# A decoder step on one core: the low parts of 44 delta net weight blocks made by an accumulating transfer from GpSimd, with other costs for transfers in the planner and the convolution states moved in fewer transfers

## The chip, the cores and the metric

One NeuronCore of one Trainium2 chip runs the whole program in one launch. TensorE (PE, with its weight loads as PEld) multiplies, VectorE (DVE) and ScalarE (ACT) do elementwise work, GpSimd (POOL) does elementwise work on data outside PSUM, and SyncE (SP) issues transfers. The five have instruction queues of their own, each in order, and wait for each other on semaphores. The metric is the device time of one execution in microseconds (us), the median of several runs; lower is better.

## The reference

A two-layer decoder trunk for a prompt of 512 tokens and 64 sample tokens (8 sequences of 8), T = 576 columns in all, with 1024 channels in fp32. Layer 0 is a pooling mixer and a SwiGLU FFN, layer 1 a gated delta net and a SwiGLU FFN; each sublayer stands between two RMS norms. What matters here is the delta net:

```python
proj = h @ w_in                      # 1024 -> 4096 (q, k, v) + 2048 (z) + 32 (b, a)
qkv_c, new_conv = short_conv(qkv, conv_buf, conv_w)     # causal, width 4, then SiLU
q, k = l2norm(...), l2norm(...)      # 8 heads of 128, each for 2 of the 16 v heads
u = solve(t_mat, v * beta[..., None])                   # unit lower triangular
w = solve(t_mat, kb * jnp.exp(gc)[..., None])
o, s_new = lax.scan(step, s0, xs)    # the state passes from chunk to chunk
o = rms_norm(o, o_norm) * jax.nn.silu(zf)
y = o.reshape(B, L, GDN_V_DIM) @ w_out                  # 2048 -> 1024
```

Beside y the delta net returns the last three rows before the convolution (new_conv) for the prompt and each sample sequence, and the recurrent states.

## The kernel before

**Weight blocks.** Every large product is made of three fp32r matmuls per pair of operands: each operand is split in a high part (rounded to fp32r) and a low part (the rest), and high x high, high x low and low x high are summed in PSUM (`mm3`, L683). A weight block is 1024 rows by 128 columns, held as 128 partitions x 8 x 128. `Weights.load` (L670) has SP fetch it from DRAM into `wraw` (512 KB); `Weights.split` (L675) has ACT copy it, rounded, into `wh`, and then one subtraction `wraw - wh` goes into `wl`, on DVE or on POOL (`EITHER`). `wraw`, `wh` and `wl` have three buffers each (`wts = Weights(ctx, 3, 3)`). One block's 48 matmuls (8 row tiles x 3 x the two halves of the columns, 256 and 320) are in the generator `halves` (L1215).

**The delta net** runs over four groups G of two k heads and four v heads. `project(G)` takes eight weight blocks (two k, two q, four v) through the matmuls, the convolution (`ac`, DVE), the activation (`ACT`) and the norms, and `zproj(h)` takes one block of z; `ZB` says which z blocks go with which group. `core(G)` forms the decay and the triangular matrices, inverts them on DVE (`inv32`, L1117: 31 rounds of a product, `ii<-ia,ii`, and a subtraction, `ii<-ii`, each of which needs the one before), scans over four spans of the prompt and updates the sample states. `out0` (L1726) multiplies the first eight v heads by eight blocks of `w_out` in pairs, beside the last core; the second half of `w_out` follows with the next norm.

**The convolution states.** `project(G)` loads the three rows before the sample tokens for its eight chunks with eight transfers into two `crow` tiles (24 rows a chunk, four chunks on 96 partitions), which PE transposes in two matmuls, and at its end PE transposes the new rows (`nct`) in two, ACT copies them to `nco`, and sixteen transfers store them, eight for the prompt and eight for the samples.

**The order of the work.** All of this is recorded as operations with dependencies, and `Plan.finish` puts them in an order for each engine: list scheduling by a rank, with costs from `Plan.cost` and the engine, port and transfer rules in `Plan.forward`, then 40 rounds in which ranks from a backward pass are stirred at random (with a fixed seed) and the best order is kept. The order is written out before the run; on the chip each engine follows its own list, so that an instruction that waits holds up all behind it on that engine. An operation of `EITHER` goes to POOL only while DVE has enough other work. A transfer cost the SP queue 60 ns there, and 2000 ns and its bytes at 240 bytes per ns to land. Since nearly all instructions are put out by one helper, the profile has one line for them (L302), and tiles are what tells them apart.

Of the kernel before, what the change touches and what calls it, by code (L numbers as in the profile page):

```python
# [11 lines left out]
F32 = mybir.dt.float32  # L12
F32R = mybir.dt.float32r
I32 = mybir.dt.int32
AF = mybir.ActivationFunctionType
ALU = mybir.AluOpType
PSUM = bass.MemoryType.PSUM
DRAM = bass.MemoryType.DRAM
SB = bass.MemoryType.SB

P = 128
D = 1024
NC = D // P
# [33 lines left out]
class Plan:  # L57
# [101 lines left out]
    def cost(self, eng, method, out, ins, k):  # L159

        n = self.size(out)
        if method == "dma_start":
            return 60.0, 2000.0 + n * list(out.ap)[0][1] * 4 / 240.0
# [194 lines left out]
    def forward(self, rank):  # L358
# [65 lines left out]
        while todo:  # L424
# [54 lines left out]
            if e == "DVE" and ops[i][8] or e == "POOL" and ops[i][9] != "memset":  # L479
                other = port["POOL" if e == "DVE" else "DVE"]  # L480
                late = max(other - 130.0 - t, 0.0)
                hold, done = hold + late, done + late
                if e == "DVE" or ops[i][9] == "tensor_tensor":
                    port[e] = t + done
# [33 lines left out]
def hybrid_kernel(  # L518
# [12 lines left out]
        ("PE", nc.tensor), ("ACT", nc.scalar), ("DVE", nc.vector), ("POOL", nc.gpsimd), ("SP", nc.sync)))  # L531
    EITHER = plan.engine(DVE=nc.vector, POOL=nc.gpsimd)
# [132 lines left out]
    class Weights:  # L665
# [3 lines left out]

        def load(self, src, row, col, nk, n=P, eng=EITHER):  # L670
            raw = self.p.tile([P, 8, P], F32, name="wraw", tag="wraw", bufs=self.raw)[:, :nk, :n]
            SP.dma_start(raw, src[row:row + nk * P, col:col + n].rearrange("(k p) m -> p k m", p=P))
            return self.split(raw, eng)

        def split(self, raw, eng=EITHER):  # L675
            _, nk, n = raw.shape
            h = self.p.tile([P, 8, P], F32R, name="wh", tag="wh", bufs=self.bufs)[:, :nk, :n]
            l = self.p.tile([P, 8, P], F32R, name="wl", tag="wl", bufs=self.bufs)[:, :nk, :n]
            ACT.activation(h, raw, AF.Copy)
            eng.tensor_tensor(l, raw, h.bitcast(F32), op=sub)  # L680
            return h, l
# [461 lines left out]
    with ExitStack() as st:  # L1143
# [80 lines left out]
        def project(G, out, zh=()):  # L1224
# [14 lines left out]
            cp = bank("x")[:, :8 * R0].rearrange("p (c r) -> p c r", c=8)  # L1239
            for j4 in range(2):  # L1240

                crow = pp.tile([4 * R0, P], F32, name="crow", tag="crow", bufs=2)
                for j, (_, _, cc) in enumerate(chunks[4 * j4:4 * j4 + 4]):
                    SP.dma_start(crow[j * R0:(j + 1) * R0],
                                 state_gdn_conv[0].rearrange("b r d -> (b r) d")[:, cc * P:(cc + 1) * P])
                PE.transpose(cp[:, 4 * j4:4 * j4 + 4].rearrange("p c r -> p (c r)"), crow, ident[:4 * R0, :4 * R0])
# [57 lines left out]
            for j, (kind, i, cc) in enumerate(chunks):  # L1304
                both = early[j:j + 1]
                yield from halves(wts.load(w_in, 0, cc * P, NC), both)
# [35 lines left out]
            nco = pp.tile([4 * R, 2, P], F32, name="nco", tag="nco", bufs=1)  # L1342
            pn_ = bank("x", (P, 4, P))[:4 * R, :2]
            for j4 in range(2):
                PE.transpose(pn_[:, j4], nct[:, 4 * j4:4 * j4 + 4].rearrange("p c r -> p (c r)"), ident)
            ACT.activation(nco, pn_, AF.Copy)
            for j, (_, _, cc) in enumerate(chunks):
                src = nco[j % 4 * R:(j % 4 + 1) * R, j // 4]
                SP.dma_start(nc_prompt[0, 0, :, cc * P:(cc + 1) * P], src[:CW - 1])
                SP.dma_start(nc_sample[0].rearrange("b r d -> (b r) d")[:, cc * P:(cc + 1) * P], src[CW - 1:])  # L1350

        def zproj(h):

            both = []
            yield from halves(wts.load(w_in, 0, CONV + h * P, NC), both)
# [370 lines left out]
        def out0():  # L1726
# [4 lines left out]
            for m0, m1 in ((0, 2), (2, 4), (4, 6), (6, 8)):  # L1731
                acs = [pp.tile([P, UTOT], F32, name="ac", tag="ac", bufs=ACB) for _ in range(m0, m1)]
                ws = [wts.load(wo, 0, m * P, 8) for m in range(m0, m1)]
# [182 lines left out]
```

## Time and profile before

| what | value |
|---|---|
| time, median of 3 runs (lowest to highest) | 1594.57 us (1593.03 to 1595.5) |
| the profiled execution: its time | 1590.5 us |
| the profiled execution: span from first to last instruction | 1588.8 us |
| first FFN and what is ahead of it | 0 to about 450 us of the span |
| delta net, groups 0 to 3 and `out0` | about 450 to 1110 us |
| second half of `w_out`, second FFN | about 1110 us to the end |
| granted TensorE clock, mean | 0.990 |

A page of the profile gives for each engine the time in which it was busy; matmuls are pipelined and their ends are modelled, so that a busy PE may still have room between two matmuls. A group's row reads: line, engine, operation, out<-in, shapes, count, then busy time and mean duration of one, then the idle time of the engine ahead of it and what ended that. The chain of waits is followed back from the last instruction: at each step to what released it, or to the instruction before it on its engine.

### The profile page before, as it was taken

How to read it: one execution, taken by the hardware profiler on the slowest of the kernel's cores; microseconds unless marked ns; L12 is line 12 of the kernel's file. 1: busy time of each engine (PE TensorE's matmuls, PEld its weight loads, DVE VectorE, ACT ScalarE, POOL GpSimd, SP SyncE). 2: the span in 40 equal slices, each digit the busy share in tenths (PEclk: the TensorE clock that was granted, in tenths of full speed). 3: DMA queues.
4: the chain of work that ended last, by engine and by line, in shares of the span. 5: the costliest groups of instructions: out<-in, count | busy, mean ns of one | idle time of the engine just before them, and what ended most of it. 6: DMA issues, size and time to landing. Idle time of an engine off the chain costs nothing.

```text
span 1588.8 us, 30549 instructions
## 1 busy us (share of the span) xinstructions
PE 1543.5 (97%) x11941; PEld 1479.0 (93%) x11941; DVE 1190.6 (75%) x2377; ACT 797.1 (50%) x1654; POOL 120.9 (8%) x257
## 2 busy tenths in 40 slices
PE   8999999999999999999999999899999999999997
PEld 8999999999999898888898889799999999999997
DVE  6894565678596798897999899658697576766864
ACT  7753443445455956353563664424465453434554
POOL 3210000000010011130211110100010000000000
PEclk9999999999999999999999999899999999999998
DMA  6454323232565432424333433555765423233263
GB/s 182 138 175 123 99 75 102 67 107 78 165 179 159 124 97 81 128 80 117 103 108 101 133 115 113 170 172 145 231 209 156 142 83 91 80 90 115 64 179 104
DMA packets 346463, 197.87 MB, mean 125 GB/s; under 512 B 14087, under 2 KB 339504, under 8 KB 346311
## 3 DMA queue, kind: packets, MB, share of 16 engines
q1 hardware_dynamic: 346319, 195.92, 42.5%
q8 instruction: 94, 1.54, 0.4%
q14 instruction: 50, 0.41, 0.1%
HBM read 165.60 MB, written 30.52 MB: 123 GB/s over the span
## 4 chain that ended last, share of the span: by engine, by line
PE 42%; DVE 16%; ACT 3%; DMA 2%; issue 2%; SPq 0%; POOL 0%; DVEq 0%; ACTq 0%
PE ps_B L302 15%; PE ps_A L302 12%; PE ps_m L302 6%; PE ps_s L302 4%; PE ps_k L302 3%; DVE ac L302 3%; DVE ii L302 2%; DVE ia L302 2%; DVE Uw L302 2%; DVE wl L302 1%; DVE vt L302 1%; PE ps_n L302 1%; DVE QD L302 1%; PE ps_x L302 1%; DVE St L302 1%
## 5 line engine op out<-in xcount | busy, mean ns | idle before, releaser
L302 ACT ACTIVATE wh<-wraw 128x1024 fp32r<-128x1024 f32 (+4 forms) x240 | 233.2, 976 | 246.1 <-PE ps_B L302 89.6
L302 DVE TENSOR_TENSOR wl<-wraw,wh 128x1024 fp32r<-128x1024 f32 (+4 forms) x233 | 259.4, 1118 | 89.9 <-ACT wh L302 42.3
L302 PE MATMUL ps_m<-hH,wh 128*128 128x320 f32 (+1 forms) x832 | 243.9, 311 | 1.2 <-ACT zz L302 0.9
L302 PE MATMUL ps_m<-hL,wh 128*128 128x320 f32 (+1 forms) x832 | 240.2, 306 | 0.0
L302 PE MATMUL ps_m<-hH,wl 128*128 128x320 f32 (+1 forms) x832 | 237.1, 306 | 0.2 <-DVE wl L302 0.2
L302 PEld LDWEIGHTS ps_m<-hH,wh 128*128 128x128 f32 x832 | 154.1, 191 | 6.8 <-issue 1.9
L302 PEld LDWEIGHTS ps_m<-hL,wh 128*128 128x128 f32 x832 | 153.5, 191 | 2.2 <-issue 0.9
L302 PEld LDWEIGHTS ps_m<-hH,wl 128*128 128x128 f32 x832 | 152.7, 191 | 2.6 <-issue 0.9
L302 PE MATMUL ps_B<-hH,wl 128*128 128x320 f32 (+1 forms) x444 | 128.9, 305 | 1.0 <-DVE wl L302 1.0
L302 PE MATMUL ps_B<-hH,wh 128*128 128x320 f32 (+1 forms) x444 | 129.3, 304 | 0.0
L302 PE MATMUL ps_B<-hL,wh 128*128 128x320 f32 (+1 forms) x444 | 128.3, 304 | 0.0
L302 PE MATMUL ps_A<-hH,wh 128*128 128x256 f32 (+1 forms) x432 | 121.1, 291 | 0.7 <-DVE yo L302 0.7
L302 PE MATMUL ps_A<-hL,wh 128*128 128x256 f32 (+1 forms) x432 | 120.8, 290 | 0.0
L302 PE MATMUL ps_A<-hH,wl 128*128 128x256 f32 (+1 forms) x432 | 120.0, 290 | 0.1
L302 PE MATMUL ps_B<-aH,wh 128*128 128x288 f32 x352 | 99.3, 296 | 1.2 <-DVE xa L302 1.2
L302 PE MATMUL ps_A<-aH,wh 128*128 128x288 f32 x352 | 99.0, 297 | 0.7 <-ACT wh L302 0.7
L302 PE MATMUL ps_B<-aL,wh 128*128 128x288 f32 x352 | 99.2, 296 | 0.0
L302 PE MATMUL ps_A<-aL,wh 128*128 128x288 f32 x352 | 99.0, 295 | 0.0
L302 PE MATMUL ps_A<-aH,wl 128*128 128x288 f32 x352 | 98.5, 295 | 0.2 <-DVE wl L302 0.2
L302 PE MATMUL ps_B<-aH,wl 128*128 128x288 f32 x352 | 98.5, 296 | 0.0
L302 PEld LDWEIGHTS ps_B<-hH,wl 128*128 128x128 f32 x444 | 81.8, 188 | 2.4 <-DVE wl L302 2.3
L302 DVE SCALAR_TENSOR_TENSOR ac<-u,cwt,ac 128x600 f32<-128x600 f32 x96 | 80.8, 851 | 2.8 <-ACT ac L302 2.5
(468 smaller groups left out, 4083.4 us busy)
## 6 DMA issues: line engine op xcount, KB each, us to landing
wraw<-in_ffn_w_in_dram SPq DMA_DIRECT2D x77, 512.0 KB
wraw<-in_gdn_w_in_dram SPq DMA_DIRECT2D x56, 512.0 KB
graw<-in_ffn_w_in_dram SPq DMA_DIRECT2D x33, 512.0 KB
wraw<-in_ffn_w_out_dram SPq DMA_DIRECT2D x32, 448.0 KB
wraw<-in_gdn_w_out_dram SPq DMA_DIRECT2D x24, 512.0 KB
wraw<-in_ffn_w_out_dram SPq DMA_DIRECT2D x32, 320.0 KB
St<-in_state_gdn_rec_dram SPq DMA_DIRECT2D x32, 256.0 KB
out_dram<-St SPq DMA_DIRECT2D x32, 256.0 KB
```

Source lines behind the costliest of these rows:

```text
L302: calls[e](*a, **k)
```

## The change

Four things are changed together.

1. `load` and `split` take `dma`. With it, `wl` is made in two steps in place of the subtraction: ACT writes `-wh` into `wl`, and a transfer issued from POOL (`SUM`) adds `wraw` to it, from SBUF to SBUF, 512 KB. It is set for the 24 blocks of `project(1)` to `project(3)`, for the z blocks 4 to 15 and for the eight blocks of `out0`: 44 blocks. Group 0, z blocks 0 to 3, the second half of `w_out` and both FFNs stay as they were. `wraw` is free for the next load only once that transfer has landed, and the matmuls that read `wl` wait for its landing.
2. `Plan.cost` gives a transfer on POOL 1200 ns of its queue and 3500 ns and its bytes at 120 bytes per ns to land; on SP 350 or 400 ns of the queue (2500 ns from DRAM to DRAM) where there were 60. In `Plan.forward` a transfer on POOL doesn't take the port that POOL shares with DVE.
3. The convolution states are loaded with three transfers a group instead of eight and stored with six instead of sixteen. They lie by 24 or 27 rows x 4 chunks x 128, so PE transposes each chunk by itself: eight matmuls in and eight out a group, where there were two and two. `crow` and `nco` share one buffer.
4. With other costs the planner finds another order for the whole program.

```diff
--- before.py
+++ after.py
@@ -160,7 +160,11 @@
 
         n = self.size(out)
         if method == "dma_start":
-            return 60.0, 2000.0 + n * list(out.ap)[0][1] * 4 / 240.0
+            m = n * list(out.ap)[0][1]
+            if eng == "POOL":
+                return 1200.0, 3500.0 + m * 4 / 120.0
+            hold = 2500.0 if out.space == DRAM and ins[0].space == DRAM else 400.0 if m > 16384 else 350.0
+            return hold, 2000.0 + m * 4 / 240.0
         ps = any(x.space == PSUM for x in ins)
         if eng == "PE":
             rows = self.rows(ins[0])
@@ -476,7 +480,7 @@
                 hold *= fast
             taken[i] = True
             todo -= 1
-            if e == "DVE" and ops[i][8] or e == "POOL" and ops[i][9] != "memset":
+            if e == "DVE" and ops[i][8] or e == "POOL" and ops[i][9] not in ("memset", "dma_start"):
                 other = port["POOL" if e == "DVE" else "DVE"]
                 late = max(other - 130.0 - t, 0.0)
                 hold, done = hold + late, done + late
@@ -529,6 +533,7 @@
     plan = Plan(tc)
     PE, ACT, DVE, POOL, SP = (plan.engine(**{name: real}) for name, real in (
         ("PE", nc.tensor), ("ACT", nc.scalar), ("DVE", nc.vector), ("POOL", nc.gpsimd), ("SP", nc.sync)))
+    SUM = plan.engine(POOL=nc.gpsimd)
     EITHER = plan.engine(DVE=nc.vector, POOL=nc.gpsimd)
     mult, add, sub = ALU.mult, ALU.add, ALU.subtract
 
@@ -667,17 +672,21 @@
             self.p = pool("wp", stack=stack)
             self.raw, self.bufs = raw, bufs
 
-        def load(self, src, row, col, nk, n=P, eng=EITHER):
+        def load(self, src, row, col, nk, n=P, eng=EITHER, dma=False):
             raw = self.p.tile([P, 8, P], F32, name="wraw", tag="wraw", bufs=self.raw)[:, :nk, :n]
             SP.dma_start(raw, src[row:row + nk * P, col:col + n].rearrange("(k p) m -> p k m", p=P))
-            return self.split(raw, eng)
-
-        def split(self, raw, eng=EITHER):
+            return self.split(raw, eng, dma)
+
+        def split(self, raw, eng=EITHER, dma=False):
             _, nk, n = raw.shape
             h = self.p.tile([P, 8, P], F32R, name="wh", tag="wh", bufs=self.bufs)[:, :nk, :n]
             l = self.p.tile([P, 8, P], F32R, name="wl", tag="wl", bufs=self.bufs)[:, :nk, :n]
             ACT.activation(h, raw, AF.Copy)
-            eng.tensor_tensor(l, raw, h.bitcast(F32), op=sub)
+            if dma:
+                ACT.activation(l, h.bitcast(F32), AF.Copy, scale=-1.0)
+                SUM.dma_start(l.bitcast(F32), raw, accum_op=add)
+            else:
+                eng.tensor_tensor(l, raw, h.bitcast(F32), op=sub)
             return h, l
 
     def mm3(ps, w, acts, nk, first=True, last=True):
@@ -1237,13 +1246,16 @@
             R0 = (CW - 1) * NB
             cst_t = pp.tile([P, 8, NB, CW - 1], F32, name="cstt", tag="cstt", bufs=1)
             cp = bank("x")[:, :8 * R0].rearrange("p (c r) -> p c r", c=8)
+            runs = ((0, 0, 2), (0, 2, 2), (1, 0, 4))
             for j4 in range(2):
 
-                crow = pp.tile([4 * R0, P], F32, name="crow", tag="crow", bufs=2)
-                for j, (_, _, cc) in enumerate(chunks[4 * j4:4 * j4 + 4]):
-                    SP.dma_start(crow[j * R0:(j + 1) * R0],
-                                 state_gdn_conv[0].rearrange("b r d -> (b r) d")[:, cc * P:(cc + 1) * P])
-                PE.transpose(cp[:, 4 * j4:4 * j4 + 4].rearrange("p c r -> p (c r)"), crow, ident[:4 * R0, :4 * R0])
+                crow = pp.tile([R0 + CW - 1, 4, P], F32, name="crow", tag="crow", bufs=1)[:R0]
+                for _, c, k in (r for r in runs if r[0] == j4):
+                    c0 = chunks[4 * j4 + c][2] * P
+                    SP.dma_start(crow[:, c:c + k], state_gdn_conv[0].rearrange("b r d -> (b r) d")[:, c0:c0 + k * P]
+                                 .rearrange("r (c p) -> r c p", c=k))
+                for c in range(4):
+                    PE.transpose(cp[:, 4 * j4 + c], crow[:, c], ident[:R0, :R0])
             ACT.activation(cst_t.rearrange("p c b r -> p c (b r)"), cp, AF.Copy)
             nct = pp.tile([P, 8, (CW - 1) * (NB + 1)], F32, name="nct", tag="nct", bufs=1)
             if G == 0:
@@ -1303,7 +1315,7 @@
 
             for j, (kind, i, cc) in enumerate(chunks):
                 both = early[j:j + 1]
-                yield from halves(wts.load(w_in, 0, cc * P, NC), both)
+                yield from halves(wts.load(w_in, 0, cc * P, NC, dma=G > 0), both)
                 psA, psB = both
                 if len(pend) == 2:
                     finish(*pend.pop(0))
@@ -1339,20 +1351,22 @@
             for f in pend:
                 finish(*f)
             R = (CW - 1) * (NB + 1)
-            nco = pp.tile([4 * R, 2, P], F32, name="nco", tag="nco", bufs=1)
-            pn_ = bank("x", (P, 4, P))[:4 * R, :2]
             for j4 in range(2):
-                PE.transpose(pn_[:, j4], nct[:, 4 * j4:4 * j4 + 4].rearrange("p c r -> p (c r)"), ident)
-            ACT.activation(nco, pn_, AF.Copy)
-            for j, (_, _, cc) in enumerate(chunks):
-                src = nco[j % 4 * R:(j % 4 + 1) * R, j // 4]
-                SP.dma_start(nc_prompt[0, 0, :, cc * P:(cc + 1) * P], src[:CW - 1])
-                SP.dma_start(nc_sample[0].rearrange("b r d -> (b r) d")[:, cc * P:(cc + 1) * P], src[CW - 1:])
+                pn_ = bank("x", (P, 4, P))[:R]
+                for c in range(4):
+                    PE.transpose(pn_[:, c], nct[:, 4 * j4 + c], ident)
+                nco = pp.tile([R, 4, P], F32, name="nco", tag="crow", bufs=1)
+                ACT.activation(nco, pn_, AF.Copy)
+                for _, c, k in (r for r in runs if r[0] == j4):
+                    cols = slice(chunks[4 * j4 + c][2] * P, (chunks[4 * j4 + c][2] + k) * P)
+                    for dst, src in ((nc_prompt[0, 0], nco[:CW - 1]),
+                                     (nc_sample[0].rearrange("b r d -> (b r) d"), nco[CW - 1:])):
+                        SP.dma_start(dst[:, cols].rearrange("r (c p) -> r c p", c=k), src[:, c:c + k])
 
         def zproj(h):
 
             both = []
-            yield from halves(wts.load(w_in, 0, CONV + h * P, NC), both)
+            yield from halves(wts.load(w_in, 0, CONV + h * P, NC, dma=h >= ZB[1]), both)
             psA, psB = both
             zz = pp.tile([P, T], F32, name="zz", tag="zz", bufs=2)
             ACT.activation(zz[:, :256], psA, AF.Silu)
@@ -1730,7 +1744,7 @@
                 yield 0
             for m0, m1 in ((0, 2), (2, 4), (4, 6), (6, 8)):
                 acs = [pp.tile([P, UTOT], F32, name="ac", tag="ac", bufs=ACB) for _ in range(m0, m1)]
-                ws = [wts.load(wo, 0, m * P, 8) for m in range(m0, m1)]
+                ws = [wts.load(wo, 0, m * P, 8, dma=True) for m in range(m0, m1)]
                 for hf in HALVES:
                     hi, o0, n = hf
                     for i in range(m1 - m0):
```

By count of the instructions in the two built programs, DVE has 114 full-size subtractions `wl<-wraw,wh` where it had 152, POOL 1 where it had 7; ACT has 44 more copies of 128x1024, and four more of 27x512 for the states; PE has 32 + 32 transposes of states where it had 8 + 8 (and 90 fill-in matmuls `ps_w` where it had 86); SP has 563 transfers where it had 623, and POOL 44 where it had none.

The order on DVE in the inversion of group 3 (`ii` is the matrix that is inverted, `ia` its transposed copy, `vs` and `vt` the v heads, `BD`, `TQ`, `ks` the samples' front), before:

```order
L302 TENSOR_TENSOR ii<-ii 128x27x3
L302 TENSOR_TENSOR TQ<-ps_k,des 64x64
L302 TENSOR_TENSOR ii<-ia,ii 128x78
L302 TENSOR_SCALAR vs<-ps_x,nk 64x128
L302 TENSOR_TENSOR ii<-ii 128x26x3
L302 TENSOR_TENSOR wl<-wraw,wh 128x1024
L302 TENSOR_TENSOR ii<-ia,ii 128x100
L302 TENSOR_TENSOR wl<-wraw,wh 128x1024
L302 TENSOR_TENSOR ii<-ii 128x25x4
```

and the same rounds in the change:

```order
L306 TENSOR_TENSOR ii<-ii 128x27x3
L306 TENSOR_TENSOR des<-des,s_in 128x128
L306 TENSOR_TENSOR ii<-ia,ii 128x78
L306 TENSOR_TENSOR vs<-vs,oss 64x512
L306 TENSOR_TENSOR ii<-ii 128x26x3
L306 TENSOR_TENSOR ii<-ia,ii 128x100
L306 TENSOR_TENSOR ii<-ii 128x25x4
L306 TENSOR_TENSOR ii<-ia,ii 128x96
L306 TENSOR_TENSOR ii<-ii 128x24x4
```

The two subtractions between the rounds are gone; the rounds follow each other.

The order on POOL from there to the end of the delta net (`nct` and `u` are the convolution's, `og` and `zz` the gated heads that `out0` and the second half read, `T`, `R`, `Rs` cleared tiles of the inversion), before:

```order
L302 TENSOR_TENSOR wl<-wraw,wh 128x1024
L302 COPY u<-cstt 128x8x3
L302 MEMSET u 128x3
L302 COPY nct<-u 128x3
L302 COPY nct<-u 128x24
L302 MEMSET R_2504 64x1024
L302 TENSOR_TENSOR hL<-og,hH 128x320
L302 TENSOR_TENSOR hL<-og,hH 128x256
L302 MEMSET Rs_2503 128x1024
L302 MEMSET T_2502 32x16x32
L302 COPY kx<-qks 128x8x8
```

and in the change:

```order
L306 DMA wl<-wraw 128x1024 x4
L306 MEMSET R_2516 64x1024
L306 TENSOR_TENSOR hL<-og,hH 128x256
L306 TENSOR_TENSOR hL<-og,hH 128x320
L306 TENSOR_TENSOR hL<-og,hH 128x256
L306 TENSOR_TENSOR hL<-og,hH 128x320
L306 TENSOR_TENSOR hL<-og,hH 128x256
L306 MEMSET Rs_2515 128x1024
L306 DMA wl<-wraw 128x1024
L306 MEMSET T_2514 32x16x32
L306 DMA wl<-wraw 128x1024 x2
L306 COPY kx<-qks 128x8x8
```

The transfers stand between POOL's other work, each behind the ACT copy that it adds to.

The order on SP at the end of the last projection, where the new convolution rows are stored, before:

```order
L302 DMA og<-og_d 128x576
L302 DMA out_dram<-nco 24x128 x6
L302 DMA z_d<-zz 128x576
L302 DMA out_dram<-nco 24x128 x2
L302 DMA out_dram<-nco 3x128 x8
L302 DMA St<-in_state_gdn_rec_dram 128x4x128 x2
```

and in the change:

```order
L306 DMA out_dram<-nco 3x256
L306 DMA out_dram<-nco 24x256 x2
L306 DMA out_dram<-nco 3x256
L306 DMA og<-og_d 128x576
L306 DMA wraw<-in_gdn_w_out_dram 128x8x128
L306 DMA og<-og_d 128x576
L306 DMA z_d<-zz 128x576
L306 DMA out_dram<-nco 24x512
L306 DMA out_dram<-nco 3x512
```

Sixteen stores became six, in two parts with a weight load of `out0` between them.

## The prediction

> **What bounds the kernel now.** I read the whole page first, then a table of stretches, then the chain of waits inside the delta net, then the groups of instructions there, and last the order in time at two places.
>
> ```profile
> span 1588.8 us, 30549 instructions
> PE 42%; DVE 16%; ACT 3%; DMA 2%; issue 2%; SPq 0%; POOL 0%; DVEq 0%; ACTq 0%
> 250.00:300.00 50.00, 50.00 (x378) 49.90 (x377) 36.14 (x55) 22.36 (x32) 0.00 (x0) 1.00 0.34 99
> 560.00:1000.00 440.00, 420.63 (x3501) 384.05 (x3499) 396.75 (x953) 216.55 (x602) 64.42 (x129) 1.00 0.38 107
> 1000.00:1110.00 110.00, 103.91 (x886) 95.37 (x887) 71.52 (x143) 42.01 (x116) 3.69 (x5) 0.95 0.55 165
> ```
>
> The stretches give busy us (and instructions) of PE, its weight loads, DVE, ACT and POOL, then clock, share of the transfer engines and GB/s. In the FFN (250 to 300) PE has 378 matmuls of 288 columns in 50 us, 132 ns each, with no gap: nothing that DVE does can shorten that stretch. In the delta net (560 to 1000) DVE is busy 396.75 of 440 us, 90%, ACT 49% and POOL 15%; the weight loads, which no longer cover each other there, drop to 87%. The order on DVE says what this means:
>
> ```profile
> 966.55 0.22 DVE L302 TENSOR_TENSOR ii<-ii 128x78 f32<-128x78 f32 x1
> 966.70 1.21 DVE L302 TENSOR_TENSOR wl<-wraw,wh 128x1024 fp32r<-128x1024 f32 x1
> 967.84 0.25 DVE L302 TENSOR_TENSOR ii<-ia,ii 128x100 f32<-128x100 f32 x1
> 968.01 1.21 DVE L302 TENSOR_TENSOR wl<-wraw,wh 128x1024 fp32r<-128x1024 f32 x1
> 969.14 0.25 DVE L302 TENSOR_TENSOR ii<-ii 128x100 f32<-128x100 f32 x1
> ...
> 981.02 0.29 DVE L302 TENSOR_TENSOR ii<-ia,ii 128x135 f32<-128x135 f32 x1
> 981.35 0.30 DVE L302 TENSOR_TENSOR ii<-ii 128x135 f32<-128x135 f32 x1
> 981.68 0.29 DVE L302 TENSOR_TENSOR ii<-ia,ii 128x126 f32<-128x126 f32 x1
> 982.01 0.29 DVE L302 TENSOR_TENSOR ii<-ii 128x126 f32<-128x126 f32 x1
> ```
>
> Bare rounds of the inversion follow each other every 0.33 us (981.02, 981.35, 981.68). With a subtraction between them the next one starts 1.29 us later (966.55 to 967.84): about 0.96 us added to a chain in which each step needs the one before. So these stretches are set by DVE's queue, and low parts stand in the middle of it.
>
> **What leaves DVE.** The built order has 38 fewer full-size subtractions on DVE and 6 fewer on POOL.
>
> ```profile
> by line: PE ps_m L302 18.4%; PE ps_s L302 10.6%; PE ps_k L302 8.2%; DVE ac L302 7.7%; DVE ii L302 6.1%; DVE ia L302 6.1%; issue 4.8%; DVE Uw L302 4.6%; DVE wl L302 3.7%; DVE vt L302 2.7%; DVE QD L302 2.2%; PE ps_x L302 2.1%; DVE St L302 1.8
> L302 DVE TENSOR_TENSOR wl<-wraw,wh 128x1024 fp32r<-128x1024 f32 x40 | 48.7, 1217 | 6.1 <-ACT wh L302 6.0
> L302 POOL TENSOR_TENSOR wl<-wraw,wh 128x1024 fp32r<-128x1024 f32 x6 | 15.3, 2546 | 19.5 <-ACT wh L302 19.5
> ```
>
> These rows are of 560 to 1090, where the 44 blocks are. Upper bound: DVE sets the pace throughout, 38 x 1.217 = 46.2 us. Lower bound of what the chain shows: 3.7% of 530 us = 19.6 us for 40 subtractions, 18.6 for 38; and nothing at all if the freed time turns into waiting. I take 25 us: the chain's 18.6 and about a quarter of the rest, since the chain names a subtraction only where no other work would have filled the place. POOL's six (2.5 us each) free POOL, which is idle anyway: nothing.
>
> **What comes to ACT, PE and SP.** 44 copies `wl<-wh` at the price of `wh`; state copies and transposes; 60 transfers fewer.
>
> ```profile
> L302 ACT ACTIVATE wh<-wraw 128x1024 fp32r<-128x1024 f32 x46 | 48.6, 1056 | 71.2 <-PE ps_m L302 57.6 <-issue 13.5
> PE 1543.5 (97%) x11941; PEld 1479.0 (93%) x11941; DVE 1190.6 (75%) x2377; ACT 797.1 (50%) x1654; POOL 120.9 (8%) x257
> L302 PE MATMUL ps_x<-ident,nct 128*108 128x128 f32 x8 | 1.8, 284 | 0.1
> L302 PE MATMUL ps_x<-ident,crow 96*128 96x96 f32 x8 | 1.4, 256 | 0.0
> L302 SPq DMA_DIRECT2D out_dram<-nco x64: 244/302/1165, 602.6 to 1018.8; - x64
> L302 SPq DMA_DIRECT2D crow<-in_state_gdn_conv_dram x32: 298/362/540, 497.4 to 771.7; - x32
> 604.97 4.15 SPq L302 DMA_DIRECT2D out_dram<-nco  x11
> SPq L302 <- DVE wl L302: 441.9, 116, 19.4
> ```
>
> ACT: 44 x 1.056 = 46.5 us, which takes it from 258.6 (216.55 + 42.01) to 305 of 550 us. Its idle time covers most of that. ACT is 3% of the chain, 48 us, for 797.1 us of work, so 6 in 100: 2.8 us, 3 with the larger `nco` copies; between 0 and, if the cover is gone because the copies stand ahead of the evacuations of PSUM, all 46.5.
>
> PE: 24 more transposes of each kind, 24 x 0.225 + 24 x 0.175 = 9.6 us; 42% of the span for 97% of busy time says 0.43 of it, 4 us (ends 0 and 9.6).
>
> SP: about 60 x 0.33 = 20 us less in its queue. Most of it is hidden: SP stands still for 441.9 us on `wl` alone, because a free `wraw` is what a load waits for, not the queue. Only the bursts of stores (4.15 us for 11) can hold up a load: I take 1 us gained (ends 0 and four bursts of 6 us). That `crow` and `nco` now share a buffer makes SP wait for the first half's stores to land before the second is copied; up to three weight blocks are on hand then, and I give it nothing. That the planner knows SP's true price (0.30 to 0.37 us, not 0.06) can help or hurt the order in any stage by a few us; I put it at zero and into the range.
>
> **What is late next: the low part itself.** The trace has no transfer from POOL. From below: a plain 512 KB load held the chain for 3.84 us; from above, twice that for its two reads, and POOL's price of the subtraction, 2.5 us, for the issue: 10.2. An accumulating transfer has to read both operands, so I take 8 us. With the copy (1.06) and without the subtraction (1.22) the low part is ready 7.8 us later than before. Does PE want it so soon?
>
> ```profile
> 727.26 3.84 DMA wraw<-in_gdn_w_in_dram
> 1043.84 1.23 DVE L302 TENSOR_TENSOR wl<-wraw,wh 128x1024 fp32r<-128x1024 f32 x1 [1.87 <-ACT wh L302]
> 1046.54 1.23 DVE L302 TENSOR_TENSOR wl<-wraw,wh 128x1024 fp32r<-128x1024 f32 x1 [0.88 <-ACT wh L302]
> 1047.35 0.40 PE L302 MATMUL ps_m<-hH,wl 128*128 128x256 f32 x2
> 1060.40 0.28 PE L302 MATMUL ps_m<-hH,wl 128*128 128x256 f32 x1
> ```
>
> Here is one of each kind: the block written at 1043.84 is first used at 1047.35, 2.3 us after its end; the one written at 1046.54 at 1060.40, 12.6 us after. A late low part of the first kind costs PE 7.8 - 2.3 = 5.5 us, because everything behind that matmul in PE's queue waits too, the core's small products among them, and DVE behind those. On average there is room: a block is 48 x 132 ns = 6.35 us of PE, and 44 blocks in 530 us is one each 12 us, so that a round of the three buffers takes 36 us and needs 6.35 + 2.1 + 8 = 16.5. The new order was made with a late low part in its costs. I take one tight block in the whole stage beyond what the order covers, rounded down: 4 us (ends 0 and eleven such blocks, 60).
>
> A price that only a page states: by the Trainium skill, "DMA: Bandwidth & Descriptors", Anatomy of one DMA, a transfer from GpSimd takes about 2.0 us plus its bytes at 436 GB/s, an estimate of 3.2 us for 512 KB. By that the low part is 3 us late, the tight block costs 0.7 us, and the sum below would be 3 us better.
>
> **Sum.** -25 + 3 + 4 - 1 + 4 = -15 us. The profiled execution's own time is 1590.5 us, 1.7 more than its span of 1588.8; it would become 1575.5. The median of the runs, 1594.57, is 4.1 above that execution, so the median becomes 1579.6, say **1579 us**. By the ends of the DVE term alone the likeliest case lies between 1566 and 1590.
>
> **Rivals.**
>
> *DVE sets the end in full* (chance 0.16): DVE's 90% is the bound, every subtraction counts. -46.2 + 3 + 4 - 1 = -40: 1554. For it: the rounds above. Against: the scans, where DVE waits for PE, and the chain, which gives `wl` only 18.6.
>
> *The freed time turns into waiting* (0.10): the chain through PE and the semaphores stays, 1591 to 1598. For it: PE is 42% of the chain, DVE 16%.
>
> *Slower: the transfer comes too late and PE's queue stops at `wl`* (0.27). One mechanism: a matmul on `wl` waits for the landing, in order. With the quoted tight block's 5.5 us it decides from four blocks on (19 us of other gain / 5.5); with a quarter of the 44 tight, 11 x 5.5 = 60, the sum is -25 + 3 + 4 - 1 + 60 = +41: 1636. For it:
>
> ```profile
> q1 hardware_dynamic: 346319, 195.92, 42.5%
> ```
>
> 195.92 MB take 42.5% of 16 engines over 1588.8 us, so 512 KB take 1.8 us of all of them. 44 transfers with two reads and a write each at up to three times that are 80 to 240 us more in 530, where the share is 0.38 to 0.55 already: at 0.8 and more, loads and low parts hold each other up, and 8 us becomes 15. Against it: the pace of one block in 12 us.
>
> The Trainium skill, same page, Issuing engines are not separate DMA queues, says that transfers of all queues run on the same 16 engines and interleave, so that another queue saves only issue time. By that rule the POOL queue brings no transfer capacity, and this rival is where it would show; no row of this trace has two queues at work to test it.
>
> **How the numbers follow.** Likeliest 0.47, in full 0.16, nothing 0.10, late 0.27. About 0.2% (3 us) is what a measurement can tell from no change. Faster: 0.47 + 0.16 and a little of the third, less what of the first ends near 1590: 0.63. Same: 0.08. Slower: 0.27 and some of the third: 0.29. The range 1550 to 1608 holds the first and third cases, nearly all of the second and the near third of the last; about 0.04 lies below it and 0.16 above.
>
> **What would show it.** Right: between 560 and 1000 DVE is busy some 40 us less and the stretch is shorter; inversion rounds follow each other without `wl`; POOL's queue of transfers appears with 44 entries of 512 KB; `wl` leaves the chain's DVE share; the time ahead of 560 and behind 1110 is as it was. Wrong: PE or its weight loads wait for a transfer into `wl`; SP waits for that transfer where it waited for DVE's `wl`; ACT's share of the chain passes 6%; DVE's share of busy time falls while the stretch keeps its length. The forecast fails if a transfer from POOL takes clearly more than 10 us under load.

## The result and the profile after

| | time, median of the runs (lowest to highest) | ratio to the kernel before |
|---|---|---|
| before | 1595.17 us (1593.03 to 1596.76), 6 runs | |
| after | 1601.09 us (1599.97 to 1607.16), 6 runs | 1.0042 [1.0029, 1.0056] |

The change made the kernel 0.42% slower, 6.7 us by the ratio. 1579 us and a gain had been forecast; the range of 1550 to 1608 holds the measured time, the direction was the other. The profiled execution of after is the slowest of the six, 6.1 us above their median, so its span shows more of a difference than the runs do.

The page of after: span, busy time of the engines, the two kinds of queues that move data, the chain of waits by engine.

```profile
span 1605.5 us, 30702 instructions
...
PE 1554.5 (97%) x11997; PEld 1490.5 (93%) x11997; DVE 1152.3 (72%) x2335; ACT 835.5 (52%) x1700; POOL 147.0 (9%) x299
...
q1 hardware_dynamic: 344759, 195.92, 42.8%
q0 software_dynamic: 6336, 23.07, 7.7%
...
PE 38%; DVE 9%; issue 3%; DMA 3%; ACT 2%; POOL 0%; SPq 0%; DVEq 0%; ACTq 0%; POOLq 0%
```

The last row can't be set beside that of before (PE 42%, DVE 16%): its shares are of the span, and the chain can be followed back to about 540 us there and only to 700 us here. Between 700 and 1110 us, where both reach, the pieces of the chain add up to these us:

| chain, 700 to 1110 us | PE | DVE | transfers | ACT |
|---|---|---|---|---|
| before | 145 | 178 | 24 | 33 |
| after | 201 | 129 | 40 | 24 |

DVE's part fell and ACT's did not rise, as hoped. That of the transfers rose by 16 us, and a queue is there that was not: q0, the 44 transfers from POOL, 23.07 MB in 7.7% of the time of 16 engines. That is 0.077 x 1605.5 = 124 us, 2.8 us of all 16 engines for each transfer, against the 1.8 that 512 KB took on the average of q1 before.

The same stretches as in the prediction, with the same columns (the last three: clock, share of the transfer engines, GB/s).

```profile
560.00:1000.00 440.00, 414.12 (x3436) 379.73 (x3435) 347.95 (x860) 245.47 (x629) 84.90 (x161) 0.98 0.60 146
1000.00:1110.00 110.00, 105.93 (x921) 96.06 (x921) 69.14 (x174) 50.13 (x125) 14.44 (x17) 1.00 0.79 209
```

DVE is busy 347.95 of 440 us where it was 396.75, 49 us less. Not all of that has left it: over the whole program its busy time fell from 1190.6 to 1152.3 us, by 38, and the rest is work that now comes later. The transfer engines went from 0.38 to 0.60, and from 0.55 to 0.79. Yet PE issued fewer matmuls in the first stretch, 3436 for 3501: the work is behind, not ahead.

DVE's transposes around the inversion of the last group (start, us, operation), from the order in time, before and then after:

```profile
950.11 4.09 DVE L302 STREAM_TRANSPOSE ia<-Uw 32x1024 f32<-32x1024 f32 x2
...
994.55 4.64 DVE L302 STREAM_TRANSPOSE Uw<-ii 32x512 f32<-32x512 f32 x4
```

```profile
981.20 8.20 DVE L306 STREAM_TRANSPOSE ia<-Uw 32x1024 f32<-32x1024 f32 x4
...
1021.75 2.35 DVE L306 STREAM_TRANSPOSE Uw<-ii 32x512 f32<-32x512 f32 x2
```

From the first `ia` to the last `Uw` the inversion takes 1024.10 - 981.20 = 42.9 us for 49.1: the relief is real where it was expected, 6 us in this group. It begins 31 us later, but that is not a loss of 31 us, since the order is another one: in `no_transfers` (below), which is level with before, the same inversion begins at 962.86, 13 us later than before, and takes 50.0. What is new on the chain of waits are longer transfers (start, us). All its transfers between 700 and 1110 us, before:

```profile
727.26 3.84 DMA wraw<-in_gdn_w_in_dram
731.78 3.00 DMA vt<-z_d
861.16 2.89 DMA vt<-z_d
930.49 3.39 DMA QD<-gc_d
1007.40 3.40 DMA og<-og_d
1019.66 3.29 DMA St<-in_state_gdn_rec_dram
1089.92 4.33 DMA og<-og_d
```

After:

```profile
744.52 3.91 DMA vt<-z_d
756.09 5.91 DMA St<-in_state_gdn_rec_dram
782.06 3.82 DMA crow<-in_state_gdn_conv_dram
868.62 4.57 DMA out_dram<-nco
888.92 7.56 DMA vt<-z_d
963.46 5.30 DMA QD<-gc_d
1046.20 5.59 DMA St<-in_state_gdn_rec_dram
1102.31 3.77 DMA og<-og_d
```

The same 256 KB of recurrent state take 5.6 to 5.9 us where they took 3.3, and z up to 7.6 where it took 3.0. Two pieces, 8.4 us, belong to the convolution states: a load of `crow` and the store that frees the buffer for the second `nco`. The transfer that the change adds is not among them. Long pieces alone don't show that its traffic is the cause: in `no_transfers` z takes 5.3 and 4.9 us on the chain, and `QD` 5.5. And DVE, which waited 21.3 us for z between 560 and 1120 before, waits 16.9 now. The runs with fewer bytes have to decide it. The rows of the added transfer itself, the issue on POOL (ns, min/median/max) and the landing (median us):

```profile
L306 POOL DMA_DIRECT2D wl<-wraw x44: 852/862/1041, 572.2 to 1080.9; - x44
```

```profile
wl<-wraw POOLq DMA_DIRECT2D x44, 512.0 KB, 5.2
```

It lands after 5.2 us, not the 8 that I took, and no row of the waits of PE or of its weight loads between 560 and 1120 names it.

### The profile page after: what moved, and what is told of

Same layout as the page of the kernel before. It is cut to its first block, busy times and chain, and to the rows that moved or that the text cites. A ratio compares the mean times of both kernels' runs of the same rounds, so it can differ in the third digit from the quotient of the medians.

```text
span 1605.5 us, 30702 instructions
## 1 busy us (share of the span) xinstructions
PE 1554.5 (97%) x11997; PEld 1490.5 (93%) x11997; DVE 1152.3 (72%) x2335; ACT 835.5 (52%) x1700; POOL 147.0 (9%) x299
## 3 DMA queue, kind: packets, MB, share of 16 engines
q0 software_dynamic: 6336, 23.07, 7.7%
## 4 chain that ended last, share of the span: by engine, by line
PE 38%; DVE 9%; issue 3%; DMA 3%; ACT 2%; POOL 0%; SPq 0%; DVEq 0%; ACTq 0%; POOLq 0%
PE ps_B L306 14%; PE ps_A L306 11%; PE ps_m L306 7%; PE ps_s L306 3%; PE ps_k L306 2%; DVE ii L306 2%; DVE ac L306 1%; DVE ia L306 1%; DVE Uw L306 1%; PE ps_x L306 1%; DMA St<-in_state_gdn_rec_dram 1%; DMA vt<-z_d 1%; DVE vt L306 1%; DVE vs L306 0%; DVE QD L306 0%
## 5 line engine op out<-in xcount | busy, mean ns | idle before, releaser
L306 DVE TENSOR_TENSOR wl<-wraw,wh 128x1024 fp32r<-128x1024 f32 (+4 forms) x195 | 212.4, 1096 | 78.8 <-ACT wh L306 24.5
L306 PE MATMUL ps_m<-hH,wh 128*128 128x320 f32 (+1 forms) x832 | 248.5, 315 | 1.6 <-ACT u L306 0.8
L306 PE MATMUL ps_m<-hL,wh 128*128 128x320 f32 (+1 forms) x832 | 246.9, 311 | 0.0
L306 PE MATMUL ps_m<-hH,wl 128*128 128x320 f32 (+1 forms) x832 | 244.8, 311 | 0.8 <-DVE wl L306 0.8
L306 PEld LDWEIGHTS ps_B<-hH,wh 128*128 128x128 f32 x444 | 82.1, 188 | 1.0 <-ACT wh L306 0.3
L306 PEld LDWEIGHTS ps_B<-hL,wh 128*128 128x128 f32 x444 | 82.2, 188 | 0.8 <-POOL hL L306 0.5
```

The lines of the kernel that those rows point to most:

```text
L306: calls[e](*a, **k)
```

## The experiments

Three theories stood after this. TRAFFIC: the transfers fill the engines on which the core's own loads run, and that eats the relief of DVE. ORDER: the other two parts of the change, and the order made with them, cost the time. CHANCE: the order search gave one kernel a lucky and the other an unlucky order. All ratios are to the kernel before, run beside on the same chip.

| run | us | ratio, 95% interval |
|---|---|---|
| no_transfers | 1594.64 | 0.9998 [0.9977, 1.0018] |
| old_order_transfers | 1651.24 | 1.0363 [1.0347, 1.0379] |
| new_order_on_dve | 1621.57 | 1.0178 [1.0160, 1.0196] |
| new_order_eighth | 1584.47 | 0.9951 [0.9933, 0.9969] |
| new_order_half | 1597.56 | 1.0023 [1.0011, 1.0034] |
| new_order_extra | 1596.26 | 1.0010 [0.9996, 1.0024] |
| no_out_transfers | 1608.34 | 1.0082 [1.0052, 1.0111] |
| traffic_in_plan | 1588.62 | 0.9970 [0.9951, 0.9990] |

**The two other parts alone.**

```diff
-            if dma:
+            if False:
```

> The changed kernel with every low part subtracted as before (no transfer from GpSimd); the scheduler's new SP costs and the new convolution states stay, and the order is made anew. Theory ORDER (the other two parts and the new order made with them cost the time; the transfers themselves gain): 1605 us or more, at least 10 above the kernel before, with DVE waiting for ps_s and ps_k in the scans as in the changed kernel. Theory TRAFFIC (the 44 transfers crowd the loads of the core's chain, the other parts are near neutral): 1590 to 1597, within 0.2% of the kernel before.

Level with the kernel before. Scheduler costs and convolution states together cost nothing that this run can tell, and ORDER in its strong form falls. (It is one order of many; how far orders differ comes below.)

**The transfers alone, in the old order.** The subtraction's place in the written order is kept; there now stand a copy on ACT and a transfer on POOL.

```diff
                 calls, _, a, k = ops[i][:4]
+                if i in self.swap:
+                    l, raw, h = self.swap[i]
+                    self.tc.nc.scalar.activation(l, h, AF.Copy, scale=-1.0)
+                    self.tc.nc.gpsimd.dma_start(l.bitcast(F32), raw, accum_op=ALU.add)
+                    continue
```

> The kernel before with its order of instructions kept word for word on every engine; only the 44 low parts of the delta net become a negative copy on ACT and an adding transfer from GpSimd, issued where the subtraction stood. Theory ORDER: the relief of DVE shows undiluted, 1570 to 1588. Theory TRAFFIC: the state loads, vt and QD are later, 1597 to 1615. Theory LATE (no order was made for the longer way, so PE stops at wl): PE and its weight loads wait for wl, 1610 or more.

58 us slower, as LATE had it. The chain of 560 to 1180 by line, and the waits of PE, SP and DVE that bear on it (us, times, longest):

```profile
by line: PE ps_m L307 22.9%; PE ps_s L307 8.9%; PE ps_k L307 8.1%; DMA wl<-wraw 7.1%; issue 6.7%; DVE ac L307 4.3%; DVE ia L307 3.9%; PE ps_x L307 2.9%; DMA vt<-z_d 2.9%; DVE Uw L307 2.4%; DVE vt L307 2.3%; DMA wraw<-in_gdn_w_in_dram 2.3%; 
```

```profile
PE ps_m L307 <- DMA wl<-wraw: 19.3, 6, 5.8
...
SPq L307 <- DMA wl<-wraw: 238.8, 39, 21.2
...
DVE vt L307 <- DMA vt<-z_d: 48.7, 7, 13.5
```

7.1% of 620 us are 44 us in which nothing but the transfer into `wl` held the chain, in eight pieces. Five of them, 24 us, lead to a matmul, which is the rival "PE's queue stops at `wl`". The other three, 19 us, lead to SP's queue, whose next load stood behind the landing; DVE waited 48.7 us for z, where before it was 21.3. So that rival is a true danger, but not the whole of the 58 us. In the new order PE has no such wait; that the landing in the planner's costs is what averts it is likely and not tested by itself.

**The new order, without the transfers.** The order of after is kept; at each transfer's place DVE subtracts, and the negative copy is left out.

```diff
+                if i in self.skip:
+                    continue
+                if i in self.swap:
+                    self.tc.nc.vector.tensor_tensor(*self.swap[i], op=ALU.subtract)
+                    continue
```

> The changed kernel with its order kept word for word on every engine; each of the 44 transfers is again a subtraction on DVE, issued at the transfer's place, and the negative copy is left out. Theory ORDER: the transfers are worth something also in the new order, so 1612 to 1640 without them. Theory TRAFFIC: without the 23 MB the loads come sooner, and the time falls to 1585 to 1597 although DVE has 44 x 1.2 = 53 us more to do.

20 us slower than after by the medians. In this order, then, the transfer is worth more than the subtraction even with its traffic. It is an upper reading of the relief, since that order was made for low parts that cost DVE nothing.

**An eighth, and a half, of the bytes in the new order.**

```diff
+                if e == "POOL" and ops[i][9] == "dma_start":
+                    a = [x[:16] for x in a]
```

> The changed kernel with its order kept; each of the 44 transfers adds only 16 of the 128 partitions, an eighth of the bytes (the low parts of the other partitions are left out of the sum). Theory ORDER: 1598 to 1603, as the changed kernel, and DVE still waits some 90 us for ps_s and ps_k between 560 and 1120. Theory TRAFFIC: 1580 to 1592, and the long pieces on the chain for St, vt and QD become shorter.

> As new_order_eighth, with 64 of 128 partitions added by each transfer (half of the bytes; the low parts of the others are left out). Theory TRAFFIC with a price in proportion to bytes: 1584.5 + (3/7) x 16.6 = 1591.6, so 1589 to 1594. A theory of a threshold (the transfers cost nothing until the engines are full): 1583 to 1587.

The eighth is 0.9951, 0.0091 or 14.5 us faster than after with the same instructions in the same order on each engine. Its queue, the pieces of `vt` and `QD` on its chain and DVE's waits between 560 and 1120:

```profile
q0 software_dynamic: 1408, 2.89, 2.5%
```

```profile
742.88 5.46 DMA vt<-z_d
...
874.91 5.07 DMA vt<-z_d
945.50 5.08 DMA QD<-gc_d
```

```profile
DVE km L308 <- PE ps_k L308: 18.9, 2, 13.4
DVE vn L308 <- PE ps_s L308: 15.3, 11, 3.5
DVE St L308 <- PE ps_s L308: 13.7, 15, 1.8
```

`St` and `crow` have left the chain, and between 700 and 1110 us its transfers add up to 23 us for 40. Those of `vt` and `QD` that stay are little shorter, so the expectation holds for `St` alone. DVE waits for PE's products just as in after, whose rows are these, and then two of before:

```profile
DVE km L306 <- PE ps_k L306: 18.9, 2, 13.4
DVE vn L306 <- PE ps_s L306: 17.9, 12, 5.0
...
DVE St L306 <- PE ps_s L306: 13.8, 15, 1.8
```

```profile
DVE vn L302 <- PE ps_s L302: 8.4, 9, 3.3
DVE St L302 <- PE ps_s L302: 7.1, 4, 4.0
```

All of DVE's waits for PE between 560 and 1120 add up to 31 us before, 90 after and 88 in the eighth. So much of the freed time did turn into waiting for PE; but it did so in the eighth too, which is 14.5 us faster, and so it does not explain why after is slower than the eighth.

What differs is how long PE stands still. Three of its waits in after, with the time and what ended each in brackets:

```profile
762.13 2.05 PE L306 MATMUL ps_k<-St,kx 128*32 128x256 f32 x32 [1.87 <-DMA St<-in_state_gdn_rec_dram]
874.01 0.66 PE L306 MATMUL ps_x<-ident,vt 128*128 128x128 f32 x4 [1.86 <-ACT nco L306]
897.38 0.66 PE L306 MATMUL ps_x<-ident,vt 128*128 128x128 f32 x4 [3.50 <-DVE vt L306]
```

The first ends with the load of `St`, the second stands behind the store of `nco` of 4.57 us, the third behind the load of z of 7.56 us. At the same matmuls the eighth waits for `St` not at all, and 1.0 us or less at the two others. Around some of the waits the granted clock is lower: from 870 to 880 us it is 0.83, and at 875 us matmuls of 256 columns start 0.21 us apart, at 879 us 0.12. The sums, in us, for the four profiled executions of this one order (`new_order_extra` follows below; a window of 10 us at clock c counts as 10 x (1 - c) lost):

| | PE's waits, 560 to 1110 us | lost to the clock, 560 to 1110 us | from the first to the last of the 44 issues on POOL |
|---|---|---|---|
| new_order_eighth | 18.6 | 1.7 | 491.8 |
| new_order_half | 26.0 | 3.4 | 501.0 |
| new_order_extra | 24.5 | 5.1 | 502.1 |
| after | 29.2 | 6.8 | 508.7 |

Of the 20.0 us by which the executions of after and the eighth differ, 16.9 lie in the stage with the transfers; PE's waits give 10.6 of them and the clock 5.1. (Before, in its own order, has 23.9 and 6.8 us.) Whether the waits bring the lower clock is not tested.

The half missed its expectation by bytes (1591.6). Its queue:

```profile
q0 software_dynamic: 3520, 11.54, 6.3%
```

Half of the bytes take 6.3% of the engines' time, where 7.7 / 2 = 3.9% would be half. By engine time (2.5, 6.3 and 7.7% of the spans: 40, 100 and 124 us) the half should stand at 0.9951 + 0.0091 x 60/84 = 1.0016, within the interval of the measured 1.0023; by bytes at 0.9990, outside it. So the price does not go by bytes. The time that the transfers hold the engines fits; but they also land later (3.4, 4.8 and 5.2 us in the eighth, the half and after), and this run can't tell the one from the other. The next one can.

**Traffic without a reader.** As the eighth, and behind each small transfer POOL issues a copy from DRAM to DRAM for which nothing waits.

```diff
+                    calls[e](*[x[:16] for x in a], **k)
+                    calls[e](self.spare[self.used % 4], self.source[self.used % 8])
```

> As new_order_eighth (the order of the changed kernel, each transfer adds 16 of 128 partitions, the rest of the low part left out), and behind each of the 44 small transfers GpSimd issues one plain copy of 512 KB from an input in DRAM to a spare place in DRAM, for which nothing waits. The low parts land early as in new_order_eighth; the traffic is back. Theory TRAFFIC (the bytes slow the other loads on the core's chain): 1594 to 1606, with St and vt pieces of 5 to 6 us on the chain. Theory LANDING (the changed kernel is slower than new_order_eighth because wl and its wraw come free later, so that SP's queue stands behind the transfer): 1582 to 1588.

9.4 us of the 14.5 came back, with the low parts about as early as in the eighth (landing after 3.5 us for 3.4), and with them `St` on the chain:

```profile
747.85 4.19 DMA St<-in_state_gdn_rec_dram
...
871.66 6.07 DMA vt<-z_d
879.73 7.53 DMA vt<-z_d
954.82 5.20 DMA QD<-gc_d
1035.29 5.11 DMA St<-in_state_gdn_rec_dram
```

This is contention by itself: copies for which nothing waits make the core's loads late; the chain's transfers are at 36 us again, and DVE's wait for z, 8.5 us in the eighth, at 17.3. POOL, which issues the copies, has no piece on the chain between 700 and 1110 us. By engine time (7.1%, 113 us) 12.6 us were due. The intervals allow for the difference (9.4 with about 3.7 to either side); a few us from the later release of `wraw`, for which SP's queue waits, are neither shown nor excluded. By the Trainium skill, "DMA: Bandwidth & Descriptors", Issuing engines are not separate DMA queues, another engine's queue adds no transfer capacity; the 9.4 us that 44 copies on POOL's queue cost here agree.

**Other seeds of the order search.**

```diff
-    ROUNDS, STIR, SEED = 40, (0.0, 0.0, 300.0, 1000.0, 3000.0), 2
+    ROUNDS, STIR, SEED = 40, (0.0, 0.0, 300.0, 1000.0, 3000.0), 3
```

> The changed kernel, with another seed of the search for an order (3 for 2); nothing else differs. Theory TRAFFIC: the transfers cost about the same in any order that was made for them, so 1594 to 1610. Theory CHANCE (the 6 us lost are one unlucky order among many that are alike): anywhere from 1578 to 1600, and more than 5 us from the changed kernel.

> The kernel before, with another seed of the search for an order (3 for 2). It measures how far two orders of one kernel lie apart: by TRAFFIC within 5 us of the kernel before, 1590 to 1600; by CHANCE 6 us or more away from it.

> The changed kernel with a third seed of the search for an order. With TRAFFIC eating the relief of DVE, the change is worth nothing on the mean of the seeds: 1588 to 1604, mean of three seeds within 5 us of that of the kernel before.

> The kernel before with a third seed of the search. 1589 to 1600, as the two others (1594.8 and 1592.6).

> The changed kernel with a fourth seed. If relief and traffic cancel: 1588 to 1602, and within 8 us of seed5_before. If the change alone costs 6 us: 1600 or more.

> The kernel before with a fourth seed: 1589 to 1605, as its three others.

> The order of seed3_after kept word for word; each of the 44 transfers adds only 16 of the 128 partitions (the low parts of the others are left out). TRAFFIC in every order: about 16 us below seed3_after (1591.4), 1572 to 1580. If the price belonged to the one order of the changed kernel: 1586 to 1592.

> The order of seed4_after kept, 16 of 128 partitions added by each transfer (the rest of the low parts left out). TRAFFIC in every order: about 16 us below seed4_after (1592.7), 1573 to 1581. If the price belonged to one order: 1587 to 1593.

| seed | before | after | after with an eighth | after, traffic in the plan |
|---|---|---|---|---|
| 2 | 1 | 1.0042 [1.0029, 1.0056] | 0.9951 [0.9933, 0.9969] | 0.9970 [0.9951, 0.9990] |
| 3 | 0.9990 [0.9977, 1.0002] | 0.9980 [0.9965, 0.9994] | 0.9882 [0.9860, 0.9904] | 0.9978 [0.9967, 0.9989] |
| 4 | 1.0066 [1.0046, 1.0087] | 0.9994 [0.9978, 1.0011] | 0.9940 [0.9920, 0.9961] | 0.9956 [0.9942, 0.9971] |
| 5 | 1.0045 [1.0024, 1.0066] | 1.0047 [1.0031, 1.0062] | | |
| mean of 2 to 4 | 1.0019 | 1.0005 | 0.9924 | 0.9968 |
| mean of 2 to 5 | 1.0025 | 1.0016 | | |

Read down a column, orders of one kernel lie 0.0076 (before) and 0.0067 (after) apart, 12 and 11 us: more than the measured effect. Two of the expectations fell to that: seed3_after is 10 us from after, as CHANCE had it, and seed4_before is above its range; seed5_after, at 1600.49 us, fits both of its theories. Read across the means, the change is worth -0.0009, -1.4 us, with a standard error of 3.9 us from the four seeds. So the 6.7 us slower are, in these numbers, -1.4 of the change, 4.0 of a before that is better than its mean and 4.1 of an after that is worse. In each of the three orders the same instructions with an eighth of the traffic's bytes are faster, by 14.5, 15.6 and 8.6 us, on the mean 12.9. The traffic's price is no matter of chance, though not the same in each order: for seed 4, 1585.31 us lie above the range expected of TRAFFIC, and below that of a price which belongs to one order. The lower clock is a part of it in all three: between 560 and 1110 it takes 6.8, 5.1 and 6.8 us with the whole traffic and 1.7 each with an eighth.

**A plan that reckons with the traffic.**

```diff
             if e == "SP":
                 dma = max(dma, t + 1400) + (done - 2000)
                 end = dma + 600
+            elif ops[i][9] == "dma_start":
+                dma = max(dma, t + 2000) + 2800
+                end = dma + 1200
```

> The changed kernel; the scheduler's model lets a transfer from GpSimd take 2.8 us of the same transfer engines that it already models for SP's transfers (before, the two did not meet in the model). Nothing else differs, the order is made anew. TRAFFIC: an order that reckons with the later loads wins back a part of the 16 us: 1585 to 1596. CHANCE: within the spread of two seeds (1591 and 1601), no better than 1590.

> traffic_in_plan with seed 3. An order that reckons with the traffic wins a part back: 1578 to 1588, below seed3_after's 1591.4. CHANCE: 1588 to 1602.

> traffic_in_plan with seed 4. An order that reckons with the traffic wins a part back: 1579 to 1589, below seed4_after's 1592.7. CHANCE: 1588 to 1602.

1588.62, 1591.63 and 1588.35 us: each faster than the kernel before with its interval below 1, and on the mean 5.9 us faster than after with the same seeds, and 8.1 us faster than before with them. Seed 3 alone is no better than seed3_after and above the range expected of a plan that wins a part back, so a lucky draw is not wholly excluded. The stretch of the delta net, with the same columns as above:

```profile
560.00:1110.00 550.00, 533.34 (x4515) 488.58 (x4514) 434.58 (x1057) 311.75 (x777) 94.51 (x175) 1.00 0.65 164
```

The transfer engines are as busy (0.65; 0.64 over the two stretches of after), but PE has done 4515 matmuls in the 550 us, where in the two stretches of after there are 4357.

**Fewer transfers.**

```diff
-                ws = [wts.load(wo, 0, m * P, 8, dma=True) for m in range(m0, m1)]
+                ws = [wts.load(wo, 0, m * P, 8) for m in range(m0, m1)]
```

> The changed kernel with transfers for the projection blocks only (28 of 44); the 16 blocks of the output product are subtracted on DVE or GpSimd as before; order made anew. Theory TRAFFIC at about 0.2 us of time for each us that the transfers take of all 16 engines (from 1584.5, 1597.6 and 1601.1 us at 2.5%, 6.3% and 7.7%): 16 x 2.8 us less gives 9 us back, and what DVE does in the output stage, where it is 63% busy, is mostly covered: 1588 to 1597. Theory that DVE's relief is worth as much in the output stage as in the rest: 1600 to 1610.

The expectation counted wrongly: `out0` has eight blocks, so 36 transfers remain. 1608 us is against TRAFFIC, which gave 4 us back for eight transfers, and in line with a relief that is worth something in the output stage too; but it is one new order, and 6 us from after is what two orders may differ by. It settles nothing.

## Why the prediction was wrong

**What was right.** DVE's queue set the inversions; its busy time fell by 38 us, for 46 us of subtractions; the inversion got shorter. ACT's 44 copies are hidden: its part of the chain between 700 and 1110 us fell, 24 us for 33. POOL's issues, 0.86 us each, are hidden too, with 1.2 us of that chain in all. The sum without its last term was -25 + 3 + 4 - 1 = -19. The means of three seeds with an eighth of the bytes stand 0.0095, 15.1 us, below those of before, with 40 of the 124 us of traffic still in them. At 12.9 us for 84 us of engine time, 0.15 for each, those 40 cost another 6: an estimate of 21 us for the change without traffic, uncertain by some 4 us from the draws of the seeds.

**Readings that were off, without turning the result.** The prediction took the page's shares of the chain as if it covered the span, but it reaches back only to 540 us. Between 560 and 1110 its pieces are 239 us of DVE, 213 of PE and 38 of ACT. So "PE is 42% of the chain, DVE 16%" says nothing for the rival of waiting, and ACT's copies would have been priced at 38 / 258.6 x 46.5 = 7 us, not 3; PE's price stays at 4. The likeliest case "between 1566 and 1590" does not follow from the ends of the DVE term: 46.2 and 18.6 in the place of 25 give 1558 and 1586. And the shared buffer of `crow` and `nco`, which was given nothing, has a store of 4.57 us on the chain and a wait of PE of 1.86 us behind it.

**The step that failed: "What is late next: the low part itself", +4 us.** It asked only whether PE waits for the landing into `wl`. PE doesn't: the landing takes 5.2 us, not 8, the order leaves room, and so that term by itself is nil. But the transfers hold 16 engines for 124 us in a stretch that also carries `St`, z and `QD`, and those loads stand on the chain of the core. Measured, that cost 12.9 us between an eighth and the whole on the mean of three orders, and 19 in all by the estimate above. The idle copies show that most of it is traffic (9.4 of 14.5 us in one order); a part from the later landing stays open. I had the number in hand, in the last rival: 80 to 240 us more of engine time in 530, loads that "hold each other up". I used it to make `wl` later, and for nothing else, and gave it to a rival instead of the sum. -21 + 19 = -2 is no proof of the split, since both numbers hold the same estimate of 6; what is measured is the -2 itself (1.0005 for 1.0019 over three seeds), the 15.1 and the 12.9.

**The term set at zero: the new order.** "Can help or hurt by a few us", put into the range. As far as four seeds can tell, it was worth 8 us in this pair (4.0 and 4.1), more than the change itself, whose -1.4 is uncertain by 3.9. That the one pair came out slower is then bad luck of the draw. The gain that would have outweighed it went to the traffic: with an eighth of it the same order stands at 0.9951.

**The rivals.** "PE's queue stops at `wl`" had the right sign and the wrong place: in the order made for it, it didn't happen; in the old one it did, as a part of 58 us; I had worked out 41. By the Trainium skill, "DMA: Bandwidth & Descriptors", Anatomy of one DMA, 3.2 us were estimated for the landing; the trace says 5.2. "The freed time turns into waiting", 1591 to 1598, is where the mean of the four seeds lies, 1597 us, but only half by its way: DVE's waits for PE did grow, by 59 us, yet by 57 in the eighth, which is faster than before. What sets after apart from the eighth are the late loads. Of the signs that I had named, two against me came true: DVE's busy time fell while the stretch did not get shorter, and SP waits for the transfer where it waited for the subtraction, 560 to 1110, after and then before:

```profile
SPq L306 <- DMA wl<-wraw: 114.7, 23, 12.5
```

```profile
SPq L302 <- DVE wl L302: 73.0, 15, 19.4
```

## What to carry to other kernels

Work that is moved from an engine to a transfer has two prices: when it lands, and how long it holds the transfer engines for everyone else; take the second in engine time, and look on the chain for the loads that share that stretch. An order kept word for word, with fewer bytes in one transfer, measures both together; idle copies beside the smaller transfers measure the second alone. Shares of a chain of waits can be compared only over a stretch that both chains reach. Where a search makes the order, measure several seeds of both kernels before a difference of half a per cent is given to the change.

## What was not expected of the hardware

A transfer that adds 512 KB from SBUF to SBUF takes 2.8 us of all 16 engines, 1.6 times the 1.8 us that the same bytes took on the average of q1 before. 64 of its 128 partitions take 0.063 x 1591.8 / 44 = 2.3 us, 81% of the whole for half of the bytes, and land after 4.8 us for 5.2; 16 partitions take 0.9 us and land after 3.4. And on the chain a load of 256 KB of states that took 3.3 us before took up to 5.9 with such transfers beside it.
